# Sum of squares of x by TensorE with an fp32 column of ones, in a two-layer encoder on one core

## The chip, the core and the metric

The kernel runs on one NeuronCore of a Trainium2 chip. Five engines work side by side, each through its own list of instructions in order: TensorE (PE; its weight loads are listed as PEld), VectorE (DVE), ScalarE (ACT), GpSimd (POOL) and SyncE (SP), which issues most of the DMAs. The metric is device time in microseconds (us), lower is better. Times within one execution are counted from the start of its span. A number such as L403 is a line of the kernel; the changed kernel is seven lines shorter, so that its L403, L411 and L436 are other lines than those of the kernel before.

## The reference, cut to what matters

One layer of the encoder begins with an RMS norm of x (1024 rows of the sequence, 1024 features) and a projection:

```python
def rms_norm(x, g):
    xf = x.astype(jnp.float32)
    y = xf * lax.rsqrt(jnp.mean(xf * xf, axis=-1, keepdims=True) + RMS_EPS)
    return (y * g.astype(jnp.float32)).astype(x.dtype)

def even_layer(x, g_pre, ...):
    h = rms_norm(x, g_pre)
    p = h @ w_in
    ...
```

So for each of the 1024 positions of the sequence the squares of its 1024 features are summed, and the inverse root of the mean scales everything that the projection makes for that position. What follows (a convolution branch, a bidirectional mLSTM, a second layer with attention and a Fourier branch) is not touched.

## The kernel before

x is read transposed: features on the 128 partitions, positions along the free axis. Two halves of 512 positions times eight blocks of 128 features give sixteen tiles `xin`. The kernel doesn't normalize x before the projection. It multiplies x by the gain g alone, splits the product into a rounded part and a remainder (ACT at L367, DVE at L368, both into tiles `pg`; PE multiplies these in three products, `mm3`, L191 to L193), and scales the results afterwards: by `rsx` where positions are on the partitions, by `rsb` where they are along the free axis.

For `rsx` the squares are needed. ACT squares each `xin` tile (L398, L401, into `xacc` and `xsq`). The seven adds of a half (L402) run on POOL for the first half and on DVE for the second, into one tile `xacc`. This is split too (`xah`, `xal`), and PE multiplies each block of 128 columns by two columns of ones: eight matmuls a half (L409, L410), which leave the sums on the partitions. DVE copies them out of PSUM (L413) and works out the inverse root in fifteen small instructions (up to L414 `rsx` and L415 `rsh`). PE then spreads `rsh` over all partitions with four fp32 matmuls against the identity (L418), and ACT stores that as `rsb` (L420).

Beside this, PE does the first projection, `v_gates`: eight blocks of 128 positions, each 8 x 3 matmuls of 272 columns (`s<-raw,pg`, `s<-wh,pg`), 192 in all; ACT and DVE evict them (L443, L444) with `rsx`. Then come the units of the convolution branch, matmuls of 512 columns, beginning with `s<-pg,wh`. That first matmul of 512 columns is used below as a landmark: everything before it is the stage that the change touches.

A scheduler sets the order of every engine's list from the program's dependencies and its own estimates; priorities in the code only lean on it. Each list is then run strictly in order, with semaphores between engines. PSUM has one buffer for the tiles `c` (L409 to L420), so that the sums and the spread of a half follow each other in it. POOL also makes the remainders of weights (L176, L205).

Of the kernel before, what the change touches and what calls it, by code (L numbers as in the profile page):

```python
# [8 lines left out]
F32 = mybir.dt.float32  # L9
F32R = mybir.dt.float32r  # L10
I32 = mybir.dt.int32
BF16 = mybir.dt.bfloat16
AF = mybir.ActivationFunctionType
ALU = mybir.AluOpType
AX = mybir.AxisListType

P = 128
# [3 lines left out]
NK = D // P  # L21
# [53 lines left out]
def hybrid_encoder(ctx: ExitStack, tc: tile.TileContext, d):  # L75
    nc = tc.nc
    V, A, PL, T = nc.vector, nc.scalar, nc.gpsimd, nc.tensor
# [3 lines left out]
    def f(ap):  # L81
        return ap.bitcast(F32)
# [18 lines left out]
    def nm(s):  # L101
        uid[0] += 1
        return f"{s}_{uid[0]}"
# [7 lines left out]
    def a_tile():  # L111

        ring[0] += 1
        if ring[0] % 3 == 0:
            return d_tile()
        return psa.tile([P, 512], F32, tag="a", bufs=2, name=nm("a"))
# [4 lines left out]
    def c_tile():  # L121
        return psc.tile([P, 512], F32, tag="c", bufs=1, name=nm("c"))
# [34 lines left out]
    def rms_scale(ss, n, width):  # L157

        v = small.tile([P, 16], F32, tag="rsin", name=nm("rsin"))[:, :n]
        V.tensor_scalar(out=v, in0=ss, scalar1=1.0 / width, scalar2=RMS_EPS,  # L160
                        op0=ALU.mult, op1=ALU.add)
        return rsqrt(v, n)
# [32 lines left out]
    def split_act_dve(hi, lo, src):  # L195
        A.activation(hi, src, AF.Copy)
        V.tensor_tensor(out=lo, in0=src, in1=f(hi), op=ALU.subtract)
# [44 lines left out]
    def op_acc(c):  # L242

        if c == 0:
            mt = [mm_tile() for _ in range(2)]
            return [mt[j // 2][:, (j % 2) * 512:(j % 2 + 1) * 512] for j in range(4)]
        return [a_tile(), a_tile(), a_tile(), c_tile()]

    def x_acc():
        return [psa.tile([P, 512], F32, tag="a", bufs=2, name=nm("x")) for _ in range(2)] + [c_tile(), d_tile()]  # L250
# [81 lines left out]
    l0a = l0.enter_context(tc.tile_pool(name="l0a", reuse_waits="tile", bufs=1))  # L332
# [2 lines left out]
    xh, xl = ([[xb[2 * half + k // 4][k % 4][i] for half in range(2)] for k in range(NK)] for i in range(2))  # L335
    rsx = l0a.tile([P, NT], F32, name="rsx")
    rsh = l0a.tile([P, NT], F32, name="rsh")
    ones2 = l0a.tile([P, 2], F32R, name="ones2")
    V.memset(f(ones2), 1.0)
    colA, colW, colD, colQ, colF = (l0a.tile([P, NT, 8], F32, name=f"col{n_}") for n_ in "AWDQF")  # L340
    gnq = l0a.tile([P, 24], F32, name="gnq")
    V.tensor_scalar(out=gnq[:, 0:16], in0=cols[:, C_GNG:C_GNG + 16], scalar1=0.5, scalar2=None, op0=ALU.mult)
# [16 lines left out]
    xp = work.enter_context(tc.tile_pool(name="l0x", reuse_waits="tile", bufs=4))  # L359
    raw = [[xp.tile([P, 512], F32, tag="xin", bufs=16, name=nm("xin")) for _ in range(NK)] for _ in range(2)]  # L360
# [33 lines left out]
    nc.sync.dma_start(out=bgate, in_=d["bgate"].broadcast_to([P, 16]))  # L394
    for half in range(2):
        hs_ = slice(half * 512, (half + 1) * 512)
        acc = xp.tile([P, 512], F32, tag="xacc", bufs=2, name=nm("xacc"))
        A.activation(acc, raw[half][0], AF.Square)  # L398
        for k in range(1, NK):
            sq = xp.tile([P, 512], F32, tag="xsq", bufs=3, name=nm("xsq"))  # L400
            A.activation(sq, raw[half][k], AF.Square)  # L401
            (PL if half == 0 else V).tensor_tensor(out=acc, in0=acc, in1=sq, op=ALU.add)  # L402
        ah_ = xp.tile([P, 512], F32R, tag="xah", bufs=2, name=nm("xah"))  # L403
        al_ = xp.tile([P, 512], F32R, tag="xal", bufs=2, name=nm("xal"))
        split_act_dve(ah_, al_, acc)
        pt = c_tile()
        for j in range(4):
            js = slice(j * P, (j + 1) * P)
            T.matmul(pt[:, 2 * j:2 * j + 2], ah_[:, js], ones2, start=True, stop=False)  # L409
            T.matmul(pt[:, 2 * j:2 * j + 2], al_[:, js], ones2, start=False, stop=True)  # L410
        ts_ = slice(4 * half, 4 * half + 4)  # L411
        ssum = small.tile([P, 4], F32, tag="oss1", name=nm("xss"))
        V.tensor_copy(ssum, pt[:, 0:8:2])  # L413
        V.tensor_copy(rsx[:, ts_], rms_scale(ssum, 4, D))  # L414
        V.tensor_scalar(out=rsh[:, ts_], in0=rsx[:, ts_], scalar1=0.5, scalar2=None, op0=ALU.mult)  # L415
        pt = c_tile()
        for j in range(4):
            T.matmul(pt[:, j * P:(j + 1) * P], rsh[:, 4 * half + j:4 * half + j + 1].broadcast_to([P, P]),  # L418
                     ident, start=True, stop=True)
        A.activation(rsb[:, hs_], pt, AF.Copy)  # L420
# [656 lines left out]
    def x1_cols(ysb, k):  # L1077

        pt = a_tile()
        for j in range(4):  # L1080
            T.transpose(out=pt[:, j * P:(j + 1) * P], in_=ysb[j][:, k * P:(k + 1) * P], identity=ident)
        return pt, cols[:, C_GPRE1 + k:C_GPRE1 + k + 1]
# [7 lines left out]
    for k in range(NK):  # L1090
        pt, g = x1_cols(ysb1, k)
# [106 lines left out]
    with tc.high_priority(offset=SPRI):  # L1198
        x1_rows(1, ysb2, ss2, xr, lambda: sp.tile([P, 1024], BF16, tag="r", bufs=2, name=nm("junk")))
        for k in range(4):  # L1200
            r21, r1 = halves(s_tile("r", F32, 2))
            pt, g = x1_cols(ysb2, k)
            A.activation(r21, pt, AF.Copy, scale=g)
            pt, g = x1_cols(ysb2, k + 4)
# [226 lines left out]
    with tc.tile_pool(name="fn", reuse_waits="tile", bufs=1) as fn:  # L1431
# [21 lines left out]
        for q in range(4):  # L1453
            if q == 2:
# [8 lines left out]
                for st in range(2):  # L1463
                    for c0, c1 in ((0, 514), (514, N_DFT)):
                        raw = wr_pool.tile([P, 1024], F32, tag="wr", name=nm("dr"))[:, 0:c1 - c0]
# [8 lines left out]
            for st in range(2):  # L1474
                pt = a_tile()
# [10 lines left out]
            if q == 0:  # L1486
                pt = a_tile()
# [3 lines left out]
        for nt in range(4):  # L1491
# [4 lines left out]
            for q, (c0, n) in enumerate(((E_CE, 258), (E_CO, 256), (E_SE, 256), (E_SO, 256))):  # L1496
                pt = a_tile()
# [30 lines left out]
    al_ = atl.enter_context(tc.tile_pool(name="atl", reuse_waits="tile", bufs=2))  # L1528
# [246 lines left out]
    with ExitStack() as os_:  # L1775
# [52 lines left out]
        def residual(half):  # L1828
            xr = [at.tile([P, S], F32, tag=tg, bufs=b_, name=nm("xr"))
                  for tg, b_ in (("acc", 1), ("mb", 1), ("es", ES_BUFS), ("zt", 1))]  # L1830
            for j in range(4):
                nc.sync.dma_start(out=xr[j], in_=x1d[4 * half + j])
            return xr

        for half, c in ((0, 0), (1, 0), (0, 1)):
            acc = x_acc() if half else op_acc(0)
# [8 lines left out]
        acc, xr = x_acc(), residual(1)  # L1845
# [143 lines left out]
```

## Time and profile before

| what | value |
|---|---|
| median of 3 runs | 1893.24 us (1891.75 to 1898.95) |
| the profiled execution | 1894.11 us, its span 1892.3 us |
| PE busy | 1802.8 us, 95% of the span |
| DVE, ACT, POOL busy | 1254.3, 664.3, 532.8 us |
| mean granted clock of TensorE | 0.972 of full speed |
| the chain that ended last | PE 82%, DVE 9%, issue 3%, DMA 3%, POOL 2%, ACT 1% |

The profile is of one execution; a busy share is of the whole span, and the first stage, some 53 us long, is under 3% of it. The granted clock is a share of 2.4 GHz and shows two levels, 1.00 and 0.50 (1.2 GHz). Matmuls are pipelined: the duration of one overlaps the next, so that the step from start to start is what one costs in a row of them.

### The profile page before, as it was taken

The page shows a single profiled execution, that of the slowest core. Times are in us where ns is not written, and L with a number is a line of the kernel's source. Part 1 is how long each engine was busy: PE and PEld are TensorE (multiplying, and loading weights), DVE is VectorE, ACT ScalarE, POOL GpSimd, SP SyncE. Part 2 cuts the span into 40 slices and gives each one's busy share as a digit, 9 for nine tenths or more (in the row PEclk, how much of TensorE's full clock was granted, in tenths as well). Part 3 has the DMA queues.
Part 4 walks back from the last instruction along what each step waited for, and adds up shares of the span by engine and source line. Part 5 has one row for each costly group of instructions (what it writes and reads, how often), then busy time and mean ns, then how long its engine had stood idle before and what let it go on. Part 6 is the DMA issues. An engine that isn't in the chain of part 4 may idle for free.

```text
span 1892.3 us, 22367 instructions
## 1 busy us (share of the span) xinstructions
PE 1802.8 (95%) x8164; PEld 1410.8 (75%) x8164; DVE 1254.3 (66%) x2119; ACT 664.3 (35%) x1051; POOL 532.8 (28%) x372
## 2 busy tenths in 40 slices
PE   6999999999999999999899699998999999999998
PEld 5988888888888877777677478876766767665786
DVE  7598759499849335776165877865567686868205
ACT  5222332422332323333245531335244454445111
POOL 3432332423241221112454433224221122103310
PEclk8999999999999999899899899999999999999999
DMA  4333222313221383558987214445300111105974
GB/s 162 119 114 114 95 65 99 127 56 106 100 92 53 126 280 121 168 181 291 309 269 265 73 50 151 167 152 196 125 17 11 65 41 53 45 34 187 326 254 156
DMA packets 144000, 256.28 MB, mean 135 GB/s; under 512 B 12881, under 2 KB 68690, under 8 KB 143762
## 3 DMA queue, kind: packets, MB, share of 16 engines
q1 hardware_dynamic: 98066, 188.06, 30.1%
q10 hardware_dynamic: 45824, 66.80, 9.6%
q8 instruction: 64, 1.05, 0.2%
q14 instruction: 46, 0.38, 0.1%
HBM read 179.64 MB, written 75.17 MB: 135 GB/s over the span
## 4 chain that ended last, share of the span: by engine, by line
PE 82%; DVE 9%; issue 3%; DMA 3%; POOL 2%; ACT 1%; SPq 0%; DVEq 0%; ACTq 0%; POOLq 0%
PE s L193 10%; PE s L191 10%; PE s L192 10%; PE mm L191 5%; PE mm L193 4%; PE mm L192 4%; PE c L1696 3%; PE d L1696 3%; PE mm L1639 2%; PE m L191 2%; PE m L192 2%; PE m L193 2%; PE p L193 2%; PE mm L1642 1%; PE o L874 1%
## 5 line engine op out<-in xcount | busy, mean ns | idle before, releaser
L614 DVE SCALAR_TENSOR_TENSOR cv<-u,cwh,cv 128x1024 f32<-128x1024 f32 x232 | 298.2, 1286 | 11.8 <-ACT cv L611 7.6
L205 POOL TENSOR_TENSOR wl<-wr,wh 128x1024 fp32r<-128x1024 f32 (+2 forms) x56 | 132.7, 2373 | 243.4 <-ACT wh L204 218.2
L191 PE MATMUL s<-qh,pg 128*128 128x512 f32 x304 | 120.4, 396 | 0.0
L193 PE MATMUL s<-qh,pg 128*128 128x512 f32 x304 | 119.8, 394 | 0.0
L192 PE MATMUL s<-ql,pg 128*128 128x512 f32 x304 | 119.0, 392 | 0.0
L205 POOL TENSOR_TENSOR ql<-raw,qh 128x1024 fp32r<-128x1024 f32 x34 | 81.4, 2400 | 105.5 <-ACT qh L204 105.5
L1679 DVE TENSOR_TENSOR e<-st,mb 128x1024 f32<-128x1024 f32 x64 | 90.5, 1463 | 28.3 <-ACT mb L1670 28.3
L1644 ACT ACTIVATE st<-mm 128x1024 f32<-128x1024 f32 x64 | 65.3, 1022 | 87.7 <-PE mm L1642 87.5
L191 PE MATMUL s<-pg,qh 128*128 128x512 f32 x240 | 95.5, 398 | 0.0
L192 PE MATMUL s<-pg,qh 128*128 128x512 f32 x240 | 95.4, 398 | 0.0
L193 PE MATMUL s<-pg,ql 128*128 128x512 f32 x240 | 95.4, 398 | 0.0
L204 ACT ACTIVATE wh<-wr 128x1024 fp32r<-128x1024 f32 (+2 forms) x56 | 53.8, 964 | 92.2 <-PE p L192 24.4
L193 PE MATMUL s<-wh,pg 128*128 128x512 f32 (+2 forms) x224 | 79.7, 360 | 3.4 <-DVE pg L368 3.4
L191 PE MATMUL s<-wh,pg 128*128 128x512 f32 (+2 forms) x224 | 80.3, 359 | 0.5 <-ACT wr L603 0.5
L1651 DVE TENSOR_TENSOR acc<-acc,mm 128x1024 f32<-128x1024 f32 x48 | 58.5, 1218 | 32.9 <-ACT st L1644 32.9
L1680 ACT ACTIVATE e<-e 128x1024 f32<-128x1024 f32 x64 | 66.0, 1057 | 38.8 <-DVE e L1679 38.2
L192 PE MATMUL s<-wl,pg 128*128 128x512 f32 (+2 forms) x224 | 79.2, 355 | 0.0
L1685 DVE TENSOR_TENSOR es<-es,e 128x1024 f32<-128x1024 f32 x48 | 71.9, 1499 | 1.1
L1696 PE MATMUL c<-e,v 128*128 128x512 f32 x128 | 68.4, 617 | 0.0
L193 PEld LDWEIGHTS s<-qh,pg 128*128 128x128 f32 x304 | 57.1, 188 | 13.1
L192 PEld LDWEIGHTS s<-ql,pg 128*128 128x128 f32 x304 | 57.1, 188 | 12.7
L1696 PE MATMUL d<-e,v 128*128 128x512 f32 x128 | 66.4, 601 | 0.0
(672 smaller groups left out, 4948.7 us busy)
## 6 DMA issues: line engine op xcount, KB each, us to landing
wr<-in_wout_dram SPq DMA_DIRECT2D x36, 512.0 KB, 5.3
yh<-ydh SPq DMA_DIRECT2D x64, 256.0 KB, 4.3
yl<-ydl SPq DMA_DIRECT2D x64, 256.0 KB, 4.4
wr<-in_w_dram SPq DMA_DIRECT2D x27, 512.0 KB, 4.3
raw<-in_wa_dram SPq DMA_DIRECT2D x22, 512.0 KB, 4.0
y1h<-ydh SPq DMA_DIRECT2D x40, 256.0 KB, 4.4
y1l<-ydl SPq DMA_DIRECT2D x40, 256.0 KB, 4.7
raw<-in_woz_dram SPq DMA_DIRECT2D x16, 512.0 KB, 4.0
```

The costliest lines, as they stand in the source:

```text
L191: T.matmul(out, lh, rh, start=start, stop=False, skip_group_check=shared)
L192: T.matmul(out, lh, rl, start=False, stop=False, skip_group_check=shared)
L193: T.matmul(out, ll, rh, start=False, stop=stop, skip_group_check=shared)
L204: A.activation(hi, src, AF.Copy)
L205: PL.tensor_tensor(out=lo, in0=src, in1=f(hi), op=ALU.subtract)
L614: tap = V.scalar_tensor_tensor(out=cv if k < TAPS - 1 else acc, in0=u[:, k:k + S], scalar=cwh[:, g, k:k + 1], in1=cv, op0=ALU.mult, op1=AL ...
L1644: A.activation(st, ps, AF.Copy)
L1651: V.tensor_tensor(out=s_["acc"], in0=s_["acc"], in1=ps, op=ALU.max)
L1679: V.tensor_tensor(out=st, in0=sc, in1=s_["mb"], op=ALU.subtract)
L1680: A.activation(st, st, AF.Exp, scale=scale)
L1685: V.tensor_tensor(out=s_["es"], in0=s_["e0"] if kt == 1 else s_["es"], in1=st, op=ALU.add)
L1696: T.matmul(s_["po"][i], v[kt // 2][:, vs], s_["e"][:, qs], start=kt == 0, stop=kt == NT - 1)
```

## The change

The adds of squares, their split and the eight matmuls of a half go. ACT writes all eight squared tiles of a half (nine buffers in place of three), and PE adds them up: for each of the four blocks of 128 positions eight fp32 matmuls with one column of ones, accumulated in PSUM, 32 a half, 64 in all. DVE reads four neighbouring columns in place of every second one. Nothing else of the program's text changes.

```diff
-    ones2 = l0a.tile([P, 2], F32R, name="ones2")
-    V.memset(f(ones2), 1.0)
+    ones1 = l0a.tile([P, 1], F32, name="ones1")
+    V.memset(ones1, 1.0)
...
-        acc = xp.tile([P, 512], F32, tag="xacc", bufs=2, name=nm("xacc"))
-        A.activation(acc, raw[half][0], AF.Square)
-        for k in range(1, NK):
-            sq = xp.tile([P, 512], F32, tag="xsq", bufs=3, name=nm("xsq"))
-            A.activation(sq, raw[half][k], AF.Square)
-            (PL if half == 0 else V).tensor_tensor(out=acc, in0=acc, in1=sq, op=ALU.add)
-        ah_ = xp.tile([P, 512], F32R, tag="xah", bufs=2, name=nm("xah"))
-        al_ = xp.tile([P, 512], F32R, tag="xal", bufs=2, name=nm("xal"))
-        split_act_dve(ah_, al_, acc)
+        sq = [xp.tile([P, 512], F32, tag="xsq", bufs=9, name=nm("xsq")) for _ in range(NK)]
+        for k in range(NK):
+            A.activation(sq[k], raw[half][k], AF.Square)
         pt = c_tile()
         for j in range(4):
-            js = slice(j * P, (j + 1) * P)
-            T.matmul(pt[:, 2 * j:2 * j + 2], ah_[:, js], ones2, start=True, stop=False)
-            T.matmul(pt[:, 2 * j:2 * j + 2], al_[:, js], ones2, start=False, stop=True)
+            for k in range(NK):
+                T.matmul(pt[:, j:j + 1], sq[k][:, j * P:(j + 1) * P], ones1, start=k == 0, stop=k == NK - 1)
         ts_ = slice(4 * half, 4 * half + 4)
         ssum = small.tile([P, 4], F32, tag="oss1", name=nm("xss"))
-        V.tensor_copy(ssum, pt[:, 0:8:2])
+        V.tensor_copy(ssum, pt[:, 0:4])
```

The scheduler makes new lists of it. POOL's list in the first stage, before (tile `xacc_319` holds the first half's sum, `wl` are remainders of weights):

```order
L402 TENSOR_TENSOR xacc_319<-xacc_319,xsq_330 128x512
L205 TENSOR_TENSOR wl_265<-wr_266,wh_264 128x544
L402 TENSOR_TENSOR xacc_319<-xacc_319,xsq_333 128x512
L402 TENSOR_TENSOR xacc_319<-xacc_319,xsq_336 128x512
L402 TENSOR_TENSOR xacc_319<-xacc_319,xsq_339 128x512
L176 TENSOR_TENSOR wl_290<-wr_288,wh_289 128x1024
L176 TENSOR_TENSOR wl_305<-wr_303,wh_304 128x1024
```

The seven adds (the last four stand here) leave; of POOL's work in this stage only the three `wl` remain.

ACT's list where the second half's squares stand, in the changed kernel (`pg` are rounded parts of x, `wr_472<-s_473` is the first eviction of the projection):

```order
L367 ACTIVATE pg_198<-xin_238,cols 128x512 [waits DMAHW4_49]
L173 ACTIVATE wh_304<-wr_303 128x1024 [waits DMAHW0_49]
L367 ACTIVATE pg_200<-xin_239,cols 128x512 [waits DMAHW5_49]
L399 ACTIVATE xsq_396<-xin_233 128x512 [waits PE_49,Activation_49]
L399 ACTIVATE xsq_397<-xin_234 128x512 [waits PE_49,Activation_49]
...
L399 ACTIVATE xsq_402<-xin_239 128x512 [waits PE_49,Activation_49]
L436 ACTIVATE wr_472<-s_473,rsx 128x256 [waits DVE_49,PE_49,Pool_49]
```

Before, these squares stood between the roundings of x. Now seven of them stand behind the last one, and each waits for PE to release a buffer of the first half's squares.

PE's list around the first half's sums, before (`ones` is the column of ones, `c_376<-cst,rsh` the spread of `rsh`):

```order
L193 MATMUL s_557<-raw_240,pg_191 128x272
L409 MATMUL c_346<-ones_204,xah_342 128x2
L410 MATMUL c_346<-ones_204,xal_343 128x2
...
L193 MATMUL s_557<-wh_264,pg_201 128x272
L418 MATMUL c_376<-cst,rsh 128x128 x4
L191 MATMUL s_584<-raw_240,pg_186 128x272
```

and in the changed kernel, the same place:

```order
L191 MATMUL s_527<-raw_252,pg_176 128x272
L403 MATMUL c_335<-ones_204,xsq_326 128x1
L403 MATMUL c_335<-ones_204,xsq_319 128x1
...
L193 MATMUL s_473<-raw_252,pg_181 128x272
...
L193 MATMUL s_554<-raw_252,pg_177 128x272
L411 MATMUL c_389<-cst,rsh 128x128 x4
L191 MATMUL s_554<-raw_252,pg_178 128x272
```

Of the first half's 32 matmuls with one column, seven stand singly or in twos among the projection's, and 25 stand in one block; 34 matmuls of the projection lie between that block and the spread. Before the spread PE has 84 of the projection's 192 matmuls in the changed kernel; before the change it had 121. The second half's 32 stand in one block, 34 matmuls ahead of the second spread. Behind the landmark the lists of both kernels are the same except for swaps of neighbours, nearly all in the mLSTM stage (667 to 935 us of the trace before) on PE, DVE, ACT and SP.

## Rows read from the trace of the kernel before

**Rows 1.** By stage: busy us (records) of PE, PEld, DVE, ACT, POOL; clock; DMA.

```profile
6.75:22.00 15.25, 13.46 (x87) 12.59 (x88) 14.10 (x11) 15.11 (x26) 12.30 (x8) 1.00 0.95 360
...
26.90:43.90 17.00, 10.90 (x43) 9.89 (x44) 13.20 (x33) 7.36 (x13) 3.04 (x1) 0.50 0.08 31
...
53.40:667.00 613.60, 613.05 (x2840) 503.92 (x2839) 445.07 (x694) 186.42 (x306) 189.27 (x118) 1.00 0.29 99
667.00:935.00 268.00, 251.76 (x1100) 195.38 (x1099) 155.20 (x505) 85.89 (x187) 54.15 (x56) 0.95 0.68 221
```

**Rows 2.** PE's waits up to 55 us: total us, times, longest.

```profile
PE s L191 <- ACT pg L367: 6.7, 1, 6.7
PE s L193 <- DVE pg L368: 6.6, 8, 2.1
PE c L418 <- issue: 2.4, 1, 2.4
PE c L410 <- DVE xal L197: 1.3, 1, 1.3
```

**Rows 3.** PE in order of time: start, us, line, form, records [idle before].

```profile
9.63 0.36 PE L191 MATMUL s<-raw,pg 128*128 128x272 f32 x1
...
39.60 2.04 PE L418 MATMUL c<-cst,rsh 128*128 128x128 f32 x8 [2.40 <-issue]
...
46.33 0.29 PE L193 MATMUL s<-wh,pg 128*128 128x272 f32 x1
46.45 0.29 PE L191 MATMUL s<-raw,pg 128*128 128x272 f32 x1
...
52.39 1.05 PE L418 MATMUL c<-cst,rsh 128*128 128x128 f32 x8
...
53.41 0.39 PE L191 MATMUL s<-pg,wh 128*128 128x512 f32 x1
```

**Rows 4.** POOL and DVE in order of time.

```profile
10.66 4.71 POOL L402 TENSOR_TENSOR xacc<-xacc,xsq 128x512 f32<-128x512 f32 x3 [1.31 <-ACT xsq L401]
...
55.47 2.40 POOL L176 TENSOR_TENSOR wl<-wr,wh 128x1024 fp32r<-128x1024 f32 x1 [23.28 <-ACT wh L173]
...
10.74 15.50 DVE L368 SCALAR_TENSOR_TENSOR pg<-xin,cols,pg 128x512 fp32r<-128x512 f32 x9
...
26.77 0.74 DVE L368 SCALAR_TENSOR_TENSOR pg<-xin,cols,pg 128x512 fp32r<-128x512 f32 x1
```

**Rows 5.** ACT's roundings and squares, and DVE's chain of small instructions.

```profile
4.88 0.88 ACT L196 ACTIVATE raw<-wr 128x816 fp32r<-128x816 f32 x1 [2.86 <-DMA wr<-in_wv_dram]
...
10.94 1.32 ACT L367 ACTIVATE pg<-xin,cols 128x512 fp32r<-128x512 f32 x2
12.17 1.14 ACT L401 ACTIVATE xsq<-xin 128x512 f32<-128x512 f32 x2
...
46.30 0.16 DVE L413 COPY xss<-c 128x4 f32<-128x4 f32 x1 [5.05 <-PE c L410]
...
49.08 0.17 DVE L415 TENSOR_SCALAR rsh<-rsx 128x4 f32<-128x4 f32 x1
```

**Rows 6.** fp32 matmuls with one column of ones elsewhere, and their stretch's clock.

```profile
1129.86 1.84 PE L1252 MATMUL p<-one,r 128*128 128x1 f32 x16
...
1135.71 1.84 PE L1252 MATMUL c<-one,r 128*128 128x1 f32 x8
...
1134.00:1137.55 3.55, 3.55 (x17) 3.55 (x18) 2.45 (x15) 0.00 (x0) 0.00 (x0) 0.50 0.45 148
```

**Rows 7.** Two waits of PE, and PE's busy us (records), clock, DMA behind each.

```profile
976.68 0.69 PE L1081 MATMUL a<-cst,th 128*128 128x128 f32 x2 [4.28 <-DVE th L1075]
...
1756.68 2.90 PE L1709 MATMUL a<-one,es 128*128 128x1 f32 x16 [3.88 <-DVE es L1685]
...
976.70:982.50 5.80, 5.80 (x20) 0.50 0.87 314
...
1757.40:1764.20 6.80, 6.80 (x22) 0.50 1.02 388
```

## The prediction

> **What bounds the kernel now.** I read the busy time by stage first. From the landmark at 53.4 us, the first matmul of 512 columns, to 667 us PE is busy 613.05 of 613.60 us [rows 1]: whatever the first stage gains or loses there is carried to 667 us whole. So the change is worth what it does to the start of that landmark, now 53.41 us [rows 3], plus what the reordered mLSTM stage makes of it.
>
> The view of PE's waits says what the first stage is short of [rows 2]. After the first 6.7 us, in which nothing is loaded, PE waits 6.6 us in eight pieces for DVE's remainders of x (L368), 1.3 us for the remainder of the sum of squares, and 2.4 us, put down to nothing, before the spread L418. All this makes 10.3 us. POOL and DVE in order of time show why DVE is late: nine remainders take 15.50 us while POOL adds, 1.72 us each, where one alone takes 0.74 us [rows 4]. POOL is busy 12.30 of the 15.25 us up to 22.00 [rows 1]. The two engines take turns. From 26.9 to 43.9 us the granted clock is 0.50, PE being busy for 10.90 us of it [rows 1]: at full clock that work would have taken half, so 5.4 us are lost to the clock. Waits and clock together cost this stage 15.7 us.
>
> **What the edits cost on PE.** The new operation is in the trace: L1252 multiplies fp32 blocks of 128 columns by one column of ones, eight matmuls in sixteen records. Sixteen take 1.84 us at full clock, with the tail of the last 0.115 us each; eight take 1.84 us at 0.50 [rows 6]. I take 0.11 and 0.22 us a record, two records a matmul. 64 matmuls are 128 records, 14.1 us at full clock. The sixteen records of L409 and L410 go, 1.8 us by the same step. PE has 12.3 us more to do, on the engine that ends the stage.
>
> The Trainium skill, in "FP8 and Floating Point Precision", section "TensorE Precision Notes", counts four passes through the array for a true fp32 matmul. By that page I'd put 64 matmuls at 28.2 us of such steps; two records a matmul is what the trace shows, and they are what I count.
>
> **What goes elsewhere.** POOL's seven adds go and three remainders of weights stay, 2.40 us for one of 1024 columns [rows 4]. DVE's seven adds and both splits go. ACT makes sixteen squares as before and two roundings fewer. Their price on the path is not their own time but when the first half's `rsh` is there, which I walk through now.
>
> **The walk to the first spread (L411).** ACT starts at 4.88 us and hardly waits up to 22 us (15.11 of 15.25 us busy [rows 1]). Up to the last rounding of x it has sixteen roundings at 0.615 us (10.94 to 12.17 for two), nine squares at some 0.53, and five roundings of weights, 4224 columns, at 0.88 us for 816 with a little overlap, some 4.4 us [rows 5]: 9.8 + 4.8 + 4.4 = 19.0, so 23.9 us. The second unit's weights are rounded one step earlier, so POOL holds their remainder from about 23.2 to 25.6, and the last two or three remainders of x queue behind it at 0.74 each: DVE is through at about 27.5. In DVE's list the copy of the sums stands behind all of these, though the sums are there sooner. The chain from it to `rsh` took 46.30 to 49.25, 2.95 us [rows 5]: `rsh` at 30.5.
>
> PE starts at 6.75. Ahead of the spread it has 84 matmuls of 272 columns at 0.12 to 0.13 us (46.33 to 46.45 [rows 3]), 10.5 us, and 64 records of the new kind, 7.0 us. Its first twelve matmuls took until 9.63 [rows 3], 1.4 us more than at that step. The waits for DVE should shrink to some 0.3. 6.75 + 10.5 + 7.0 + 1.4 + 0.3 = 26.0. PE then stands still from 26.0 to 30.5: the wait for `rsh` takes the place of the removed ones. Behind the spread in PE's list stand 108 matmuls of the projection that could have run, but the list is strictly in order. ACT's evictions L436 wait for the same `rsx`, as before the change, only sooner; ACT's other work is done by then, since the seven squares behind the last rounding find their buffers free (the 25-matmul block ends 34 matmuls, 4.3 us, before 26.0) and end near 27.6.
>
> **From the spread to the landmark.** 108 matmuls at 0.125, 13.5 us; the second half's 64 records, 7.0 us; two spreads at 1.05 us [rows 3], 2.1 us. 30.5 + 22.6 = 53.1, against 53.41: at full clock the change is worth -0.3 us. The second spread waits for nothing: 4.3 us of matmuls stand ahead of it, against the chain's 2.95.
>
> **The clock.** Behind PE's wait of 4.28 us the clock is 0.50 over the next 5.80 us, and behind that of 3.88 us over 6.80 us [rows 7], with PE busy all the time. A wait of 4.5 us should cost the same: 5.8 to 6.8 us of work at 0.50, half of it lost, 2.9 to 3.4. I take 3.1. Whether the clock also falls in the block of 32 one-column matmuls no row shows: all such blocks in the trace are at most sixteen records long at a stretch of full clock, against 64 here. From below it costs nothing; from above half the block runs at 0.50 (another 3.5 us) and 3.2 us of work behind it (1.6 lost), 5.1 us. A row leans to the dear side: from 1134.00 to 1137.55 PE was busy throughout, nearly all with one-column matmuls, and the clock stayed at 0.50 [rows 6]. In that case the first block would be slowed too, which fills PE's wait instead of adding to it. I take 1.0.
>
> The Trainium skill ("TensorE: Matmul & The Clock Gate", "Part 1: The HAM clock gate") says that the clock follows how busy PE has been recently; taken plainly, a block that keeps PE busy would hold the full clock, and the 1.0 would be 0. The stretch of rows 6, busy and still at 0.50, doesn't agree with that plain reading.
>
> **The sum.** -0.3 + 3.1 + 1.0 = +3.8 us at the landmark, carried to 667 us. In the mLSTM stage neighbours are swapped; PE is idle there 16.2 of 268 us and the mean clock is 0.95 [rows 1]. One wait of some 4 us with its stretch of low clock more or less makes 4 to 7 us; I expect 0, with 3 us either way. The profiled execution took 1894.11 us, 0.87 above the median 1893.24. 1894.1 + 3.8 = 1897.9, against the median 1897.0 us.
>
> **The rivals.**
> - *No clock is lost* (chance 0.13): `rsh` comes earlier or the low stretch is short, and the landmark moves by -3 to +0.8. For it: the waits for DVE go with POOL's adds. Against it: every wait of this length that I looked at was followed by a low clock [rows 7]. Even with all 15.7 us regained, 12.3 of new work leave only -3.4. Time: 1890 to 1894.
> - *Both blocks run at 1.2 GHz* (0.10): the clock falls early in each and stays down behind it. The first block takes 14.1 in place of 7.0 and PE reaches the spread at 33.1, behind an `rsh` at about 32; then 22.6 + 7.0 at the second block, 62.7, and 3 us of loss behind: +12, so 1905. It decides, and the kernel is slower, from 9.5 us of loss on. For it: the stretch of rows 6; against it: sixteen records at full clock in the same rows.
> - *Four passes after all* (0.03): the one-column matmul takes 0.44 us here. The first block then needs 7.0 more, of which 4.5 fall into the wait, the second 7.0 more: +9.5 on the forecast, 1906.5. The rows of L1252 speak against it; it is the page's rule on fp32 above.
> - *The reordered mLSTM stage gains or loses over 9.5 us* (0.03 for a gain, 0.02 for a loss): two or three of its waits go or come.
> - The forecast itself has the rest, 0.69, with a range of its own from 1893 to 1901.
>
> **The numbers.** About 0.5%, 9.5 us, is what a measurement of this kernel can tell from no change. Faster: 0.03. Slower: both blocks slow, four passes, a loss later, less what of these stays under 9.5 us: 0.13. Same: 0.84. The range 1890 to 1904 leaves out the slow rivals and the tails.
>
> **What would show it.** In the changed profile: DVE's remainders of x at 0.74 us except beside POOL's three; the last one near 27.5 us; PE's waits for L368 under 1 us in sum and one wait of 4 to 5 us before L411 near 30.5; 128 records of L403 at 0.11 us a step; a clock of 0.50 behind that wait; the landmark near 57 us and the stage behind it as before. I'm wrong if PE doesn't wait before L411, if a matmul of L403 steps by more than 0.25 us at full clock, or if the landmark moves as said and the end doesn't.

## The result, and the profile after

The changed kernel takes 1905.44 us (median of 5 runs, 1902.08 to 1907.34) against 1893.63 of before beside it: a ratio of 1.0059 with a 95% interval of 1.0048 to 1.0070. That is 11.2 us by the ratio and 11.8 us between the medians. A second series gave 1906.81 and 1.0069 (1.0050 to 1.0087). It is slower by 0.6%, beyond the noise, and outside the forecast range of 1890 to 1904. The profiled execution took 1907.34 us, its span 1905.5.

The view by stage, where it answers to [rows 1]; the columns are the stretch, its length, busy us (records) of PE, PEld, DVE, ACT and POOL, the granted clock, the DMA share and GB/s:

```profile
6.75:21.70 14.95, 14.95 (x109) 14.95 (x110) 10.47 (x15) 14.50 (x25) 2.10 (x2) 1.00 0.97 346
21.70:28.50 6.80, 6.80 (x32) 6.80 (x32) 6.73 (x8) 6.18 (x11) 4.58 (x2) 0.50 0.01 4
28.50:38.70 10.20, 9.10 (x78) 8.91 (x76) 2.91 (x17) 2.43 (x6) 0.00 (x0) 1.00 0.19 67
38.70:49.00 10.30, 10.30 (x50) 10.30 (x50) 2.51 (x16) 0.47 (x1) 0.00 (x0) 0.50 0.09 38
49.00:58.35 9.35, 9.35 (x77) 9.35 (x76) 1.07 (x5) 1.55 (x3) 0.00 (x0) 1.00 0.08 24
```

PE was busy for all of the 14.95 us before 21.70, and the clock fell to 0.50 all the same. Before 38.70 it had been busy for 7.7 us, since its last wait ended at 30.95. The 1.00 of the first row is not right for its first part: the trace has no record of the clock before 11.43 us, and the view counts such time as full clock. PE in order of time shows that a matmul of 272 columns stepped by 0.23 us there and by 0.12 behind it:

```profile
10.87 0.43 PE L191 MATMUL s<-raw,pg 128*128 128x272 f32 x1
11.10 0.43 PE L192 MATMUL s<-raw,pg 128*128 128x272 f32 x1
...
11.63 0.29 PE L191 MATMUL s<-raw,pg 128*128 128x272 f32 x1
11.75 0.29 PE L192 MATMUL s<-raw,pg 128*128 128x272 f32 x1
```

So the first 4.7 us of PE's work ran at 0.50 too. In [rows 1] the same holds up to 9.78 us, which the prediction's 1.4 us for the first twelve matmuls allows for. PE's waits up to 60 us, for [rows 2]:

```profile
PE s L191 <- ACT pg L367: 6.7, 1, 6.7
PE c L411 <- issue: 1.1, 1, 1.1
```

The 10.3 us of waits behind the first are down to 1.1. The two low stretches together are as long as the one before, 17.1 us, but PE was busy for only 10.9 us of that one and is busy for all of these: 8.5 us are lost in place of 5.4. PE in order of time, for [rows 3] (start, us, line, form, records):

```profile
16.78 6.14 PE L403 MATMUL c<-ones,xsq 128*128 128x1 f32 x49
...
30.95 1.13 PE L411 MATMUL c<-cst,rsh 128*128 128x128 f32 x8 [1.10 <-issue]
...
35.19 10.40 PE L403 MATMUL c<-ones,xsq 128*128 128x1 f32 x64
...
51.39 1.05 PE L411 MATMUL c<-cst,rsh 128*128 128x128 f32 x8
...
58.35 0.40 PE L191 MATMUL s<-pg,wh 128*128 128x512 f32 x1
```

The clock fell 4.9 us after the first block began and 3.5 us after the second did. The second took 10.40 us in place of 7.0. The landmark stands at 58.35, 4.94 later (57.74, 4.33 later, in the second profile). DVE, POOL and the chain to `rsh`, for [rows 4, 5]:

```profile
16.38 4.64 DVE L368 SCALAR_TENSOR_TENSOR pg<-xin,cols,pg 128x512 fp32r<-128x512 f32 x6 [0.93 <-ACT pg L367]
21.53 6.46 DVE L368 SCALAR_TENSOR_TENSOR pg<-xin,cols,pg 128x512 fp32r<-128x512 f32 x4 [0.50 <-ACT pg L367]
27.91 0.15 DVE L406 COPY xss<-c 128x4 f32<-128x4 f32 x1
...
30.68 0.17 DVE L408 TENSOR_SCALAR rsh<-rsx 128x4 f32<-128x4 f32 x1
```

```profile
24.47 2.96 POOL L176 TENSOR_TENSOR wl<-wr,wh 128x1024 fp32r<-128x1024 f32 x1 [1.15 <-ACT wh L173]
```

Six remainders in 4.64 us are 0.77 each; the last four take 6.46 beside POOL's `wl`. `rsh` is there at 30.85, as walked through (30.5).

Behind the landmark more is lost. To find where, I matched PE's instructions of both traces and took the median difference of their starts (after minus before, us): +5.0 at 56 to 66 us, +7.9 at 640 to 666, +10.2 at 940 to 970, +11.6 at 1200, +13.2 at 1840. In the second profile these are +4.4, +5.9, +9.2, +11.5 and +12.5. Each compares one execution with one, and the two differ by 2.0 us at 640. The step before 640 is one wait, by PE's waits from 60 to 130 us of after, and the low stretch behind it:

```profile
PE s L191 <- ACT wr L596: 1.9, 1, 1.9
```

```profile
93.50:96.80 3.30, 1.42 (x11) 1.42 (x12) 3.23 (x3) 2.15 (x4) 2.12 (x1) 0.99 0.00 0
96.80:100.20 3.40, 3.40 (x18) 3.40 (x17) 3.29 (x4) 0.00 (x0) 0.28 (x1) 0.50 0.53 154
```

Before the change the same wait was 0.5 us, with no low clock behind it:

```profile
PE s L191 <- ACT wr L603: 0.5, 1, 0.5
```

In the second profile it was 2.0 us, again with no low clock behind it. The second half of the mLSTM stage, first of before and then of after, the same work in each:

```profile
846.00:935.00 89.00, 78.14 (x335) 61.30 (x334) 42.64 (x135) 26.01 (x56) 22.43 (x14) 0.94 0.88 291
```

```profile
852.40:945.00 92.60, 80.38 (x337) 62.43 (x337) 44.17 (x134) 25.99 (x56) 22.83 (x14) 0.93 0.83 275
```

3.6 us more: PE idle for 12.2 us in place of 10.9, and busy for 2.2 more.

### The profile page after: what moved, and what is told of

Read it like the earlier page. It is cut to its first block, busy times and chain, and to the rows that moved or that the text cites. A ratio compares the mean times of both kernels' runs of the same rounds, so it can differ in the third digit from the quotient of the medians.

```text
span 1905.5 us, 22562 instructions
## 1 busy us (share of the span) xinstructions
PE 1819.9 (96%) x8276; PEld 1426.9 (75%) x8276; DVE 1243.7 (65%) x2110; ACT 663.2 (35%) x1049; POOL 518.7 (27%) x365
## 4 chain that ended last, share of the span: by engine, by line
PE 82%; DVE 7%; DMA 4%; issue 2%; POOL 2%; ACT 1%; SPq 0%; ACTq 0%; DVEq 0%; POOLq 0%
PE s L191 11%; PE s L193 11%; PE s L192 10%; PE mm L191 4%; PE mm L193 4%; PE mm L192 4%; PE c L1689 3%; PE d L1689 3%; PE mm L1632 2%; PE m L193 2%; PE m L191 2%; PE m L192 2%; PE mm L1635 1%; PE o L867 1%; PE p L193 1%
## 5 line engine op out<-in xcount | busy, mean ns | idle before, releaser
L607 DVE SCALAR_TENSOR_TENSOR cv<-u,cwh,cv 128x1024 f32<-128x1024 f32 x232 | 298.1, 1285 | 12.5 <-ACT cv L604 8.3
L193 PEld LDWEIGHTS s<-qh,pg 128*128 128x128 f32 x304 | 57.1, 188 | 13.3
L191 PEld LDWEIGHTS s<-qh,pg 128*128 128x128 f32 x304 | 57.1, 188 | 12.1
```

What stands on the lines that cost most here:

```text
L191: T.matmul(out, lh, rh, start=start, stop=False, skip_group_check=shared)
L193: T.matmul(out, ll, rh, start=False, stop=stop, skip_group_check=shared)
L607: tap = V.scalar_tensor_tensor(out=cv if k < TAPS - 1 else acc, in0=u[:, k:k + S], scalar=cwh[:, g, k:k + 1], in1=cv, op0=ALU.mult, op1=AL ...
```

## The experiments

The first theory: a block of one-column matmuls lowers the clock although PE is busy. Its rival: the records cost what they cost, and the clock falls behind waits. The second: the new order of the mLSTM stage costs 3 to 5 us by itself. Its rival: a late first stage loses more later, whatever the order. The third concerns the wait at 90 us. A shift is the median difference of starts against before, as above; "the median stands ... above" is against the runs of before on the same chip.

**Seven eighths of the new matmuls left out** (one_mm). Only k = 7 is summed.

```diff
-            for k in range(NK):
-                T.matmul(pt[:, j:j + 1], sq[k][:, j * P:(j + 1) * P], ones1, start=k == 0, stop=k == NK - 1)
+            for k in (NK - 1,):
+                T.matmul(pt[:, j:j + 1], sq[k][:, j * P:(j + 1) * P], ones1, start=True, stop=True)
```

> Of the eight matmuls that sum a block of positions only the last is left (eight in all, 16 records in place of 128): seven eighths of the squares are left out of the sum. This takes away 112 records, 12.3 us at full clock, and the dense blocks of one-column matmuls; POOL stays free. Behind the landmark PE's list is that of the kernel before, the mLSTM stage included. Both theories on the blocks: PE has 102 matmuls ahead of the first spread, 6.75 + 12.8 + 0.9 + 1.4 = 21.9, waits 8.6 us for rsh at 30.5, then 90 matmuls, 0.9 and 2.1 of spreads, 44.8, and 3 us lost to the clock behind the wait: landmark near 48 (41 if the clock holds). Theory 'the reordered mLSTM stage costs the last 4 to 5 us': with the order of before the shift at the end equals the shift at 100 us within 1.5 us, time about 1893.6 - 5 + 2 = 1890. Rival 'any shift of the first stage costs later, whatever the order': the end is 4 us or more above the shift at 100 us, 1895 or more.

The landmark came at 43.1 us, and the kernel took 1885.12 us, a ratio of 0.9948 (0.9935 to 0.9960). The landmark came 5 us sooner than worked out: with no block ahead of it the copy of the sums stands before DVE's last remainders, so the spread starts at 25.57 and PE waits 1.9 us. The shift is -10.3 at the landmark and -7.3 at 640 us, and the median is 9.6 below that of before: with before's order nothing more is lost behind 640 us. It has 16 records, as many as before: freeing POOL and DVE of the adds is worth 10 us at the landmark, and the other 112 records take 15 (12.3 at full clock).

**The second spread put back** (spread_back).

```diff
+        with tc.high_priority(offset=-200 if half else 0):
             pt = c_tile()
             for j in range(4):
                 T.matmul(pt[:, j * P:(j + 1) * P], rsh[:, 4 * half + j:4 * half + j + 1].broadcast_to([P, P]),
                          ident, start=True, stop=True)
```

> The changed kernel with the second spread (L411) put back to where it stood before, 8 matmuls ahead of the landmark in place of 48; all else in PE's list is that of the changed kernel. Theory 'the place of the second spread delays the release of the weight tiles, the chain ACT, POOL, DMA that follows, and PE at 90 us': landmark 58.4 as in the changed kernel, PE's wait before ACT's wr at 90 us 0.5 us in place of 1.9, no stretch of 0.50 at 97 us, shift at 100 us +5 to +6 in place of +7.7, time 1903. Rival 'the place of the spread does nothing, the weights come late because the whole stage is': shift at 100 us +7.7 still, time 1905.4.

The kernel took 1906.56 us, 1.0066 (1.0054 to 1.0079). PE's wait at 90 us:

```profile
PE s L191 <- ACT wr L597: 2.1, 1, 2.1
```

The theory on the spread's place falls. The low stretches became 10.2 us each (20.5 to 30.7 and 41.0 to 51.2), and the landmark 59.71. In the other kernels told of here that wait was anything from 0 to 3.1 us, and 0.6 and 2.0 in two that only add matmuls to the kernel before. The one with 2.0 (order_of_before) has before's own list of PE behind the landmark, so this wait is no property of the changed list. What sets it is open.

**The same 64 matmuls, spread out** (interleaved). After the first eight, which come in one block at 8.5 us, mostly one or two stand between three matmuls of the projection; the second half's sums go to a PSUM buffer that is free at the time, and spreads and evictions are placed anew.

```diff
+                for half in range(2):
+                    for _ in range(Q[half].get(tt, [0] * NK)[k]):
+                        sum_mm(half, done[half])
+                        done[half] += 1
```

> The same 64 fp32 matmuls with one column, 128 records, but one or two at a time between the projection's matmuls in place of blocks of 25 and 32 (the second half's sums take a free PSUM buffer). Theory 'dense blocks of one-column matmuls lower the clock': clock 1.00 from 10 us up to the landmark, no wait before the first spread, 6.75 + 192 x 0.125 + 14.1 + 2.1 + 1.4 + 0.5 = 48.8, so a landmark of 48.5 to 51. Rival 'the records cost the time wherever they stand' (the clock falls with the share of one-column matmuls, or the records cost more than 0.11 us): landmark 55 to 59. The mLSTM stage is reordered more than in the changed kernel: the end is not forecast better than landmark shift +-6 us: 1889 to 1896 by the theory, 1898 to 1909 by the rival.

The kernel took 1892.63 us, 0.9988 (0.9978 to 0.9998): faster than before by a hair, with all 128 records. The first stage and pieces of PE in order of time:

```profile
6.75:51.00 44.25, 44.25 (x328) 44.25 (x329) 22.72 (x59) 24.24 (x43) 6.46 (x3) 1.00 0.41 151
```

```profile
17.32 0.43 PE L191 MATMUL s<-raw,pg 128*128 128x272 f32 x1
17.55 0.40 PE L192 MATMUL s<-raw,pg 128*128 128x272 f32 x1
...
17.92 0.29 PE L191 MATMUL s<-raw,pg 128*128 128x272 f32 x1
18.04 0.29 PE L192 MATMUL s<-raw,pg 128*128 128x272 f32 x1
...
24.44 0.28 PE L408 MATMUL c<-ones,xsq 128*128 128x1 f32 x2
24.58 0.37 PE L191 MATMUL s<-wh,pg 128*128 128x272 f32 x1
24.79 0.28 PE L192 MATMUL s<-wl,pg 128*128 128x272 f32 x1
24.91 0.29 PE L193 MATMUL s<-wh,pg 128*128 128x272 f32 x1
25.04 0.50 PE L408 MATMUL c<-ones,xsq 128*128 128x1 f32 x4
...
51.03 0.40 PE L191 MATMUL s<-pg,wh 128*128 128x512 f32 x1
```

PE is busy for 44.25 of 44.25 us. The 1.00 of the row is again not right for its start: the trace's first record of the clock is at 17.78, and up to there the matmuls of 272 columns stepped by 0.23 us. I had expected 1.00 from 10 us on; why the low clock of the start lasted longer here than before (9.78) is open. From 17.78 on, for 33 us in which 112 of the 128 records stand among wide matmuls, PE is as busy as in the changed kernel's blocks, and the clock does not fall. The theory on blocks holds against its rival.

**Squares in the projection's type** (f32r_blocks), one record a matmul:

```diff
-        sq = [xp.tile([P, 512], F32, tag="xsq", bufs=9, name=nm("xsq")) for _ in range(NK)]
+        sq = [xp.tile([P, 512], F32R, tag="xsq", bufs=9, name=nm("xsq")) for _ in range(NK)]
-                T.matmul(pt[:, j:j + 1], sq[k][:, j * P:(j + 1) * P], ones1, start=k == 0, stop=k == NK - 1)
+                T.matmul(pt[:, 2 * j:2 * j + 2], sq[k][:, j * P:(j + 1) * P], ones1, start=k == 0, stop=k == NK - 1)
```

> The squares rounded by ACT to the type of the projection's operands, two columns of ones: 64 records in place of 128, blocks of 25 and 32 records in place of 50 and 64. Theory 'dense blocks lower the clock': half as long, they lower it for less; PE waits 6 us for rsh at 30.5 and loses 3 us behind it: landmark 50 to 52. Rival 'every block of such matmuls lowers the clock, whatever its length': landmark 53 to 55. Time 1893.6 + (landmark - 53.4) +- 4: 1890 to 1897.

The landmark came at 49.69, just under what the theory gave, and the kernel took 1893.81 us, 0.9998 (0.9988 to 1.0007). The second block, and the stretches before and after the clock falls in it:

```profile
33.39 4.92 PE L403 MATMUL c<-ones,xsq 128*128 128x2 f32 x32
```

```profile
33.40:35.50 2.10, 2.10 (x22) 2.10 (x20) 0.00 (x0) 0.00 (x0) 0.00 (x0) 0.99 0.76 250
35.50:42.30 6.80, 6.80 (x32) 6.80 (x32) 2.74 (x17) 0.47 (x1) 0.00 (x0) 0.50 0.01 2
```

The drop is no matter of fp32: 32 records of the other type bring it too, although the clock had only come back at 32.06 from a fall at 28.64, behind a wait of 2.8 us. The block of 25 at 16.7 us did not bring it.

**Only the first half by PE** (first_half_only), and **only the second** (second_half_only). The other half keeps the adds of before.

```diff
+        if half == 0:
+            sq = [xp.tile([P, 512], F32, tag="xsq", bufs=9, name=nm("xsq")) for _ in range(NK)]
...
+        else:
             acc = xp.tile([P, 512], F32, tag="xacc", bufs=2, name=nm("xacc"))
```

> Only the first half's squares are summed by PE in fp32 (32 matmuls, 64 records, a block of 50 among them); the second half is added up by DVE as before. Theory 'a block of one-column matmuls lowers the clock while PE is busy': the clock falls once, near 22 us, inside the block, for about 6.8 us (3.4 lost), and not again: 110 matmuls, 64 records and 1.4 make 29.2, with the loss 32.6 at the first spread, no wait there, then 82 matmuls, 16 records and 2.1 of spreads: landmark 46 to 48. Rival 'the clock falls only behind a wait, or with both blocks': no stretch of 0.50 that begins in the block; rsh at 30.5 and 14.2 behind: landmark 44 to 45.5. Time 1894.7 and the shift of the landmark, +-4: 1884 to 1892. PE's list in the mLSTM stage is reordered more (556 rows moved against before, 283 in the changed kernel).

> Only the second half's squares are summed by PE in fp32, in a block of 32 matmuls, 64 records; the first half is added up by POOL as before. Theory: the clock falls inside the block, PE busy, 3 to 5 us after it began, and stays low behind it: with the waits of before ahead of the first spread, 53.4 + 5.2 (48 records more) + 5 (the loss) = 63, or up to 4 less since DVE has no adds: landmark 59 to 64. Rival 'the block costs its records': no low stretch begins inside it, landmark 55 to 58.5. Time 1898 to 1906.

With the first half alone the landmark came at 49.10, and the kernel took 1897.70 us, 1.0020 (1.0011 to 1.0030). With the second half alone these are 60.51 and 1910.24 us, 1.0083 (1.0070 to 1.0096). The clock around the first half's block, then the second half's:

```profile
17.00:20.50 3.50, 3.50 (x34) 3.50 (x32) 3.50 (x5) 3.50 (x7) 0.62 (x1) 1.00 1.05 350
20.50:30.70 10.20, 10.20 (x48) 10.20 (x48) 9.69 (x12) 7.86 (x13) 4.84 (x2) 0.50 0.03 10
```

```profile
36.40:43.20 6.80, 6.80 (x61) 6.80 (x59) 0.70 (x3) 1.30 (x3) 0.00 (x0) 1.00 0.45 155
43.20:56.80 13.60, 13.60 (x63) 13.60 (x64) 2.96 (x18) 1.01 (x3) 0.00 (x0) 0.50 0.01 1
```

Each block lowers the clock by itself, with PE busy ahead of it; the first half's stretch was longer than I said. Both medians stand 7 to 8 us above the landmark's shift. Both expected times failed, 1884 to 1892 and 1898 to 1906: 3.8 us of the excess lie between 100 and 640 us in each, told under the last heading.

**The first half by fours, the second in a block** (first_half_spread): as in the interleaved kernel, but four matmuls after each three of the projection's, and the changed kernel's list behind. Twenty of the first half's 32 stand so, from 24.3 us on; eight stand in a block at 9.2 us, four at 22 to 24.

> All 64 fp32 matmuls, the first half's by fours between three matmuls of the projection, the second half's in one block of 32 as in the changed kernel; behind the landmark PE's list is the changed kernel's, row for row. Theory on the clock: no low stretch ahead of the first spread, one that begins inside the second half's block and ends behind it: 31.5 at the end of the first spread, 72 matmuls, 10.4 for the block, 1.6 behind, 1.05: landmark 53 to 54.5. Rival 'so many one-column matmuls lower the clock wherever they stand': two low stretches, landmark 57 to 59. Theory 'the changed kernel's order of the mLSTM stage costs 3 to 5 us by itself': the end stands 3 us or more above the shift at 100 us. Rival 'the order costs nothing, a late first stage does': within 1.5 us of it. Time 1897 by the first, 1894 by the second.

The landmark came at 60.79, later than either expectation, and the kernel took 1906.35 us, 1.0064 (1.0049 to 1.0079).

```profile
22.00:29.20 7.20, 7.20 (x64) 7.20 (x64) 6.84 (x5) 5.93 (x11) 4.62 (x2) 1.00 0.00 0
29.20:36.00 6.80, 6.80 (x32) 6.80 (x32) 3.73 (x21) 2.19 (x5) 0.00 (x0) 0.50 0.00 1
36.00:42.80 6.80, 6.80 (x60) 6.80 (x58) 0.01 (x1) 0.60 (x1) 0.00 (x0) 1.00 0.44 157
42.80:56.50 13.70, 13.70 (x65) 13.70 (x64) 2.98 (x18) 0.84 (x2) 0.00 (x0) 0.50 0.00 0
```

Fours are too many: the clock falls twice, against my expectation and as its rival said. This sets the theory right in one point: not the unbroken block matters but how thickly such matmuls stand. Against the interleaved kernel, with the same 128 records, there are 20.5 us of 0.50 more in these two stretches and 2.2 us fewer at the start (up to 15.5 in place of 17.8). Half of the 18.3 us is 9.1, and the shift at 56 to 66 us is 8.8 us larger (+7.4 against -1.4).

**Three kernels on the order behind.** Matmuls whose results are written over are added to the kernel before. Twenty ahead of the second half's sums make the scheduler choose the changed kernel's mLSTM order; ten, or twenty of fp32, ahead of the first half's leave before's. (PE's list of the late one differs from before's up to 150 us: its second spread, 1.05 us, stands behind the landmark.)

```diff
+            for _ in range(20 if half == 1 and j == 0 else 0):
+                T.matmul(pt[:, 2 * j:2 * j + 2], ah_[:, js], ones2, start=True, stop=True)
```

> The kernel before with twenty matmuls of its own kind (xah by two columns of ones, the result written over) added ahead of the second half's sums: 20 records, 2.2 us. Its first stage is that of before but for them; by them the scheduler comes to the mLSTM order of the changed kernel (11 rows of PE's list differ behind the landmark, against 283 between the changed kernel and before). Landmark 53.4 + 2.2 = 55.6 at full clock, up to 60 if the block of 28 lowers the clock. Theory 'the changed order of the mLSTM stage costs 3 to 5 us by itself': the median stands 2.5 to 5 us above that of before plus the shift at 100 us. Rival 'the loss behind 100 us belongs to the changed first stage': within 1 us of it.

> The kernel before with ten such matmuls ahead of the first half's sums: 10 records, 1.1 us, at a place where PE waits 2.4 us for rsh a little later; every list of the kernel behind them stays as it was. Both theories: landmark shift 0 to 1.1, more by up to 3 if the stretch of 0.50 gets longer; the median stands within 1 us of that of before plus the shift at 100 us. If it stands 2.5 us or more above, the place of a loss behind 100 us says nothing of the order.

> The kernel before with twenty fp32 matmuls of one column (40 records, their results written over) added ahead of the first half's sums: a first stage about as late as the changed kernel's, with before's own order from the mLSTM stage on. Their records stand where the granted clock of before is 0.50: 0.22 us each, 8.8, or 4.4 where it is 1.00: landmark shift +4.4 to +9. Theory 'the changed order of the mLSTM stage, not the late first stage, costs what is lost behind the landmark': the median stands within 2 us of that of before plus the landmark's shift. Rival 'a late first stage loses more later, whatever the order': 3.5 us or more above it, as in the changed kernel.

> The changed kernel once more, for a second profile. If its losses belong to the order of its lists, they stand at the same places: landmark +4.9 +-0.3, low clock inside both blocks, a shift 3 to 5 us larger behind the mLSTM stage (from 950 us on) than at 660 us, median 1904 to 1907. PE's wait at 90 us has been between 0.5 and 2.1 us in kernels with the same weights in the same order; if it comes out near 0.5 here, it is no property of the change.

The medians are, in this order, 1902.83 us, 1.0042 (1.0028 to 1.0057); 1895.41, 1.0009 (1.0001 to 1.0018); 1893.75, 0.9999 (0.9988 to 1.0010); and the changed kernel again 1906.81. In order_of_after the block is of 28 records of 128x2 from 45.5 us on; the clock fell at 48.1, with PE busy, and the landmark came at 58.88. The changed kernel's second profile has its landmark 4.33 later (+4.9 +-0.3 was expected) and loses 3.3 us more behind the mLSTM stage. The late one was not late: its 40 records took 8.53 us, but PE's waits of 1.3 and 2.4 us went and 2.0 us of those for DVE, the low stretch ended at 41.2 in place of 43.9, the second spread left the stage, and the shift at 56 us was +0.1. So it could not try the rival with a late first stage. All kernels with one of the two orders of the mLSTM stage, in us:

| kernel | mLSTM order | shift at 640 us | at 940 | at 1840 | median over before |
|---|---|---|---|---|---|
| changed | changed | +7.9 | +10.2 | +13.2 | +11.8 |
| changed, again | changed | +5.9 | +9.2 | +12.5 | +12.5 |
| spread_back | changed | +8.0 | +11.9 | +14.9 | +11.9 |
| first_half_spread | changed | +8.9 | +10.9 | +13.2 | +11.6 |
| order_of_after | changed | +5.5 | +5.6 | +4.7 | +8.9 |
| one_mm | before | -7.3 | -10.4 | -12.9 | -9.6 |
| order_of_before | before | +4.1 | +4.3 | +1.3 | +1.5 |
| late_order_before | before | -0.6 | -2.8 | +0.5 | -0.6 |

The median over before less the shift at 640 us is +2.7 to +6.6 with the changed order and -2.6 to 0.0 with before's; in the five kernels here with a third order it is 0.1 to 4.0. This figure sets one execution against medians, and its scatter is large: the -2.6 is order_of_before's, whose list of PE behind the landmark is before's own, and within 1 us was expected. Still it speaks for the order. Lateness alone does not do it: second_half_only is the latest of all at 640 us (+14.1) and has 1.4 by this figure, and order_of_after and order_of_before, nearly as late as each other (+5.5 and +4.1), end 7.4 us apart in their medians. And order_of_after, whose first stage is that of before but for one block, goes with it in its median. Its profile does not: that execution lost nothing behind 640 us, and its six runs fall into 1897.2 to 1900.4 and 1905.2 to 1906.0. So the order is supported, not settled; a kernel as late as the changed one in before's order was not found.

**A version meant to beat both** (f32r_first_half): the first half's squares in the projection's type, 32 records; the second half's adds on DVE.

```diff
+        if half == 0:
+            sq = [xp.tile([P, 512], F32R, tag="xsr", bufs=8, name=nm("xsq")) for _ in range(NK)]
...
+                    T.matmul(pt[:, 2 * j:2 * j + 2], sq[k][:, j * P:(j + 1) * P], ones2, start=k == 0, stop=k == NK - 1)
```

> A version meant to beat both: the first half's squares summed by PE in the projection's type, one record a matmul (32 records, none of the adds of POOL), the second half added up by DVE as before (16 records). 120 matmuls and 32 records stand ahead of the first spread, so that PE arrives at 6.75 + 15.0 + 3.5 + 1.4 = 26.7 and waits 1 to 3.5 us for rsh at 27.6 to 30.2; 72 matmuls, 16 records and 2.1 behind it: landmark 41 to 44 at full clock, 3 more if the clock falls behind the wait. Rival 'the time comes back in a wait of PE for weights at 80 to 90 us': the shift at 100 us is less than half that of the landmark. Time 1884 to 1889, by the rival 1889 to 1892.

The kernel took 1891.93 us, 0.9984 (0.9974 to 0.9994), 3 us less than before; 1884 to 1889 was expected. The landmark came at 45.27, not at 41 to 44: the second half's adds got in among DVE's remainders, and PE waited for one:

```profile
PE s L193 <- DVE pg L368: 4.8, 2, 4.5
```

The clock fell within this wait, at 27.7, and was 0.50 up to 34.5. The shift was still -6.8 at 640 us, so that the rival's loss at 80 to 90 us is not what took the gain; the medians differ by 2.8. The order is a third one, and where the rest went was not tried.

## Why the prediction was wrong, point by point

In the profiled execution the kernel ends 13.2 us later than before, 9.4 more than the 3.8 of the sum. Of these, 1.1 lie at the landmark, 3.0 between it and 640 us, and 5.3 behind 640 us. The experiments show the cause of the first; the causes of the other two stay open.

- **Records, waits, the walk to the spread.** Right. 128 records, two a matmul, 0.11 us a step at full clock; no wait for DVE's remainders, `rsh` at 30.85 (30.5 forecast). The Trainium skill's four passes ("FP8 and Floating Point Precision", "TensorE Precision Notes") do not show as records: the block of 25 matmuls at 16.78 has 49 or 50, not 100. Whether one record holds two passes the trace can't tell; its step of 0.11 us is what the sum needed.
- **The step that failed first: "I take 1.0" for the clock in the block of 32, and 3.1 behind PE's wait.** The clock fell inside the first block already. 6.8 us at 0.50 lost 3.4, which filled most of the wait of 4.5. The low clock of the start lasted 1.65 us longer than before (0.8 lost), the 0.3 of waits did not come, and the spread started 0.45 later than the 30.5 of the walk: 4.5 - 3.4 - 0.8 + 0.3 + 0.45 = 1.05, against 1.1 measured. So the 3.1 was never paid. The second block and what followed ran 10.3 us at 0.50: 5.15 lost, the upper bound of 5.1 that I had worked out and set aside. -0.3 + 0 + 5.15 = 4.85, against 4.94 measured. The sum of 3.8 came near by two errors of opposite sign, which is luck.
- **"I'm wrong if PE doesn't wait before L411."** It did wait, for 1.1 us in place of 4.5, so this sign did not come. The last one did: the landmark moved nearly as said (+4.94), and the end did not (+13.2).
- **The Trainium skill on the clock, weighed on the wrong side.** The Trainium skill ("TensorE: Matmul & The Clock Gate", "Part 1: The HAM clock gate") ties the clock to how busy PE has been. Busy time as the profile counts it was 100% in both blocks, for all of PE's work ahead of the first and for 4.2 us ahead of the second, and the clock fell. The trace disagrees with the plain reading; the one row that had said so [rows 6] deserved the weight, and I moved only 1.0 of 5.1 towards it.
- **"Carried to 667 us whole."** Failed, by 3.0 us in one profile and 1.6 in the other: a wait at 90 us grew from 0.5 to 1.9 or 2.0, and once the clock fell behind it. What sets that wait is open. That PE was busy for nearly all of the stage told nothing of how closely ahead of it the weights arrive.
- **The mLSTM term, "0, with 3 us either way".** Behind 640 us the two profiles lose 5.3 and 6.6, the largest part of the miss. The 0 had no reason behind it but that neighbours only change places, and the bound of 3 was too narrow: with the changed order kernels lie 2.7 to 6.6 above their shift at 640 us. That the order does it is supported, not shown; how it would do so stays open.
- **The rivals.** "Both blocks run at 1.2 GHz" named the time, 1905, and half the mechanism: the clock fell in both, but only 4.9 and 3.5 us in, and the first loss cost nothing. Its +12 at the landmark was +4.9. A time that fits is no proof of its path.

## What to carry to other kernels

Handing adds to TensorE as one-column matmuls cost more here than their records: where they stood thickly, the granted clock fell for the matmuls behind them too. Put them by ones and twos among wide matmuls, or where PE would wait anyway. And where a scheduler orders the program, a small edit at the front can come with a loss far behind it as large as at its place (5.3 us against 4.9 here); compare the order of the later stages, and measure with that order held, before crediting the edit.

## What the runs showed of the hardware that was not expected

- The granted clock falls to 0.50 in a stretch where PE is never idle: in both blocks of the changed kernel, and in 32 matmuls of 128x2 in the projection's type. With one or two such matmuls between three of 272 columns it stays at 1.00, for the 33 us behind 17.8 in the interleaved kernel; with four it fell at 29.2.
- PE starts at 0.50, and how long that lasts differs from kernel to kernel though PE is busy: up to 9.8 us before, 11.4 in the changed kernel, 17.8 in the interleaved one. The views print 1.00 for it; the step of the matmuls of 272 columns, 0.23 us in place of 0.12, tells.
- Work in front of a wait can be free: forty records, 8.53 us of PE, left the shift behind the landmark at +0.1 us, since two waits, part of a low stretch and a spread went from ahead of it.
- In first_half_only and second_half_only PE loses 3.8 us between 100 and 640 us with no wait, at full clock. The stretches with nearly the same work, before and first_half_only:

```profile
107.00:660.00 553.00, 553.00 (x2480) 450.58 (x2479) 412.32 (x648) 167.71 (x279) 164.10 (x107) 1.00 0.28 95
```

```profile
104.00:660.00 556.00, 556.00 (x2475) 449.86 (x2474) 411.23 (x646) 168.04 (x279) 163.71 (x107) 1.00 0.29 94
```

  The median step from a matmul `s<-ql,pg` to the next is 226 ns in before, the changed kernel and all others here, and 232 in these two. They keep the tiles of both methods, which may put later tiles elsewhere in SBUF; but f32r_first_half keeps tiles of both too, and its step is 226. The cause is open.
